# Another order of heads and channel groups by the column tiles of their weights, in a hybrid decoder layer on one core

## The chip, the cores and the metric

The kernel runs on one core of a Trainium2 chip. The metric is the time of one execution on the device in microseconds. A time of 2246.14 us is the median of three runs of the kernel before the change. The profile is of one more execution.

## What is computed

One layer takes 1024 new positions of one sequence and one new position each of 8 others, 2048 wide. With `h = rmsnorm(x) * (1 + scale) + shift`, where scale, shift and gate come from a conditioning vector through `w_ada`, it does this, cut from the reference:

```python
z = h @ w_in                                   # 2048 -> 8208 columns
b_a, c_a, h_a, g_a, qkv, g_b, beta_logit, alpha_logit = jnp.split(z, SPLIT_POINTS, axis=-1)
conv_out, new_a_buf = causal_depthwise_conv(c_a * h_a, conv_a_buf, conv_a_w)
y_a = b_a * conv_out * jax.nn.silu(g_a)
qkv_c, new_qkv_buf = causal_depthwise_conv(qkv, conv_qkv_buf, conv_qkv_w)
qkv_c = jax.nn.silu(qkv_c).astype(f32)
...
o, s = gated_delta_rule(q, k, v, g, beta, s0)
o = rmsnorm(o, o_norm_g).reshape(bsz, t, D_GDN).astype(x.dtype) * jax.nn.silu(g_b)
y = jnp.concatenate([y_a, o], axis=-1) @ w_out
return x + gate * y, new_a_buf, new_qkv_buf, s.astype(s0.dtype)
```

There are 8 channel groups of 128 columns (the first part, y_a) and 8 heads of 128 (the delta rule). Everything is in fp32 and the states are outputs too.

## The kernel before

**Columns.** A column tile is 128 columns of `w_in`, and its product over 2048 rows is one column of work. Group g needs four: C, H, gate and B, at 1024, 2048, 3072 and 0, plus 128 g. Head h needs four parts: k, q, v and gate, at 5120, 4096, 6144 and 7168, plus 128 h. All these bases are multiples of 1024, so all four columns of group or head i have the same place i modulo 8 within a block of eight tiles. In this text they are "of tile i". There are 64 such columns in each half.

**Halves.** The 1024 positions are done in two halves of 512; the second takes the 8 single positions along. In each half come the input products, then the output products with `w_out`, 16 column tiles. Half 0 begins with a ramp: while scale and shift are computed from `w_ada`, the first seven columns are multiplied as their inputs become ready. These are head 0's four and group 0's C, H and gate. Six of them are loaded two at a time in pieces of 128 KB (`add_pair`, L570), the seventh, the gate (`RONE`, L1364), as four pieces of 256 KB.

**A weight's way.** `Stream` (L557 and on) has one list, `todo`, of quads: 512 rows of one column, 256 KB, in runs of 512 bytes. For each quad the SP queue issues the load into `raw`; ACT rounds it to `whi`; POOL, or VectorE if POOL is busy, writes the rest `wlo`; then TensorE does three matmuls for each of its four tiles. Four raw buffers and four split ones (RAW, SPL, L387) let a load be issued up to eight quads ahead of its product. The order of `todo` is the order of the products.

**Heads.** A head's delta rule runs beside the products as a chain: preparation (`gdn_prep`, which loads `dA` by DMA), inversion (`gdn_invert`: ACT's `sp`, products, and through DRAM `ub` and `tb`, then 31 steps on VectorE), and application (`gdn_apply`, with `pb`, `u`, `st`, four chunks one after another). One head's inversion waits for the one before it, and so does its application. At most three heads have buffers for k and q.

**What sets the order of instructions.** The program is written out by a planner when it is built. `_Order` keeps an estimated time of every engine, tile and transfer; a generator that waits is resumed when the estimate says that its data are there, and its instructions are put at that place into the engines' queues. All queues then run in that order, whatever the true times are. Transfers are estimated by `_transfer` (L293): 210 GB/s for runs of 128 elements, for every column alike. The order of heads and groups is made by `order(half)` (L1338) from `GROUPS` and `APART`. Before the change, with C and H written CH and gate and B written GB, the columns are, in half 0 after the ramp: group 0's B, head 1, group 7 CH and GB, head 2, group 1 CH, head 3, group 1 GB, head 4, group 2 CH, head 5, group 2 GB, group 3 CH, head 6, group 3 GB, then head 7's four parts with two columns of groups 4 and 5 between them, then group 5 GB and group 6. In half 1: head 0, group 0 CH, head 1, group 0 GB, group 7 CH, head 2, group 7 GB, head 3, group 1, and then as in half 0.

**Gates.** `gate_chunks` (L1516) computes the third part of the `w_ada` product beside half 0's products, in steps at least `GATES` apart; its loads are `gw`, 256 KB each, on the same SP queue. A step was placed when its two tiles were estimated to have landed.

Of the kernel before, what the change touches and what calls it, by code (L numbers as in the profile page):

```python
# [11 lines left out]
ALU = mybir.AluOpType  # L12
# [4 lines left out]
P = 128  # L17
# [5 lines left out]
NH = 8  # L23
NC = 4
# [354 lines left out]
def _trunk(ctx, tc, nc, xT, w_in, w_ada, w_out, pack, consts, vecs, csq, ssm, yT, cap, cqp, ssp, cas, cqs, sss):  # L379
# [411 lines left out]

    solved, merged, recd = [0, 0], [0, 0], [0, 0]

    def gdn_prep(half, h, gp, t):
# [4 lines left out]
        g4 = {n: gt[n][:, h, :] for n in gt}  # L799
# [5 lines left out]
        SY.dma_start(dA[:], gcd[half, h * NC:(h + 1) * NC, :].partition_broadcast(P))  # L805
# [105 lines left out]
        yield LANDED  # L911
        cx["yc"] = yc

    def gdn_apply(half, h, gp, done, cx, kq, yt):
# [3 lines left out]
        g4 = {n: gt[n][:, h, :] for n in gt}  # L918
# [61 lines left out]
        for c in range(NC):  # L980
            col = slice(c, c + 1)
            oc = po[:, c * P:(c + 1) * P]
            zero = half == 0 and c == 0
            if zero:
                r = vn[:, c, :]
                G.memset(os_[:, c, :], 0.0)
            else:
                pks = ch_tile()
                mm(pks[:, :P], kT[c], st[h][:], start=True, stop=True)
                mm(pks[:, P:2 * P], qT[c], st[h][:], start=True, stop=True)  # L990
# [12 lines left out]
            pd = ch_tile()  # L1003
            mm(pd[:, :P], kt[:, c, :], u2[:], start=True, stop=True)
            if zero:
                V.tensor_copy(st[h][:], pd[:, :P])
            else:
                V.scalar_tensor_tensor(st[h][:], st[h][:], g4["egl"][:, col], pd[:, :P], ALU.mult, ALU.add)
            yield [st[h][:], u1[:], MARGIN]
            mm(oc, dA[:, c, :], u1[:], start=True, stop=True)  # L1010
        recd[half] = h + 1
        od.unpin(cx["v"])
        if half:
            SY.dma_start(ssp[h], st[h][:])


        yield [po[:]]
# [20 lines left out]
        done.append(h)  # L1038


    sample_done = []
# [296 lines left out]
    def order(half):  # L1338

        a = [("a", i) for i in GROUPS for _ in range(2)]
        every = (0, 1, 2, 3)
        r = [] if half == 0 else [("h", 0, every)]
        if half == 0:
            a.pop(0)
        for h in range(1, NH):
            for _ in range(APART[half][h - 1]):
                r.append(a.pop(0))
            if h < NH - 1:  # L1350
                r.append(("h", h, every))
                continue
            for part in every:
                r += [("h", h, (part,)), a.pop(0)]
        return r + a

    GROUPS = (0, 7, 1, 2, 3, 4, 5, 6)

    APART = ((1, 2, 1, 1, 1, 2, 1), (1, 2, 1, 2, 1, 2, 1))

    HCOLS, ACOLS = (5120, 4096, 6144, 7168), (1024, 2048, 3072, 0)
    ADA = 9

    RCOLS, RONE = ((ACOLS[0], ACOLS[1]), (HCOLS[0], HCOLS[1]), (HCOLS[2], HCOLS[3])), ACOLS[2]  # L1364
    for kp in range(NK // 2):
        for c in RCOLS:
            ws.add_pair(w_in, c, kp)
        if kp % 2:
            ws.add(w_in, RONE, (kp // 2,))
    for half in range(2):  # L1370
        seen = [0] if half == 0 else []
        for kind, i, *parts in order(half):
            if kind == "h":
                cols = [HCOLS[part] for part in parts[0]]
            else:
                cols = ACOLS[2 if half or i else 3:] if i in seen else ACOLS[:2]
                seen.append(i)
            for c in cols:
# [137 lines left out]
    def gate_chunks():  # L1516
# [11 lines left out]
        for f in range(NK):  # L1528
# [2 lines left out]
                od.pin(ps)  # L1531
            for i in (4 * f, 4 * f + 2):
                yield GATES
                yield [tiles[i][:], tiles[i + 1][:]]
                for k in range(i % 4 * 4, i % 4 * 4 + 8):
                    j = k % 4
                    mm(ps[32 * j:32 * j + 32, f % 4 * P:(f % 4 + 1) * P], sc[:, k, :],
                       tiles[f * 4 + k // 4][:, j * P:(j + 1) * P], cost=0.096 if k % 8 else 0.18,
                       start=(k < 4), stop=(k >= 12), tile_position=(0, 32 * j))
                tiles[i] = tiles[i + 1] = None  # L1540
                for j in (4, 5):
                    if i + j < 4 * NK:
                        load(i + j)
# [41 lines left out]
    for half in range(2):  # L1585
# [3 lines left out]
        with ExitStack() as pools:  # L1589
# [7 lines left out]
            def chain(h, half, queue, done, gp):  # L1597

                while len(queue) <= h or len(queue[h]["ready"]) < 2 or recd[half] < h - 1:
                    yield 0.2  # L1600
                t = queue[h]
                yield [t["kq"][:], MARGIN]
                cx = yield from gdn_prep(half, h, gp, t)
                yield from gdn_invert(half, h, gp, t["kq"], cx)
                yield from gdn_apply(half, h, gp, done, cx, t["kq"], t["gb"])

            def runner(zl, queue, done, gp, half):
                yield from gates(half, zl)
# [6 lines left out]
            def head(i, parts, pss=None):  # L1615
                for part in parts:
                    if part == 0:
                        while recd[half] < i - 2:
# [5 lines left out]
                    t = queue[i]  # L1624
# [4 lines left out]

            groups = {}  # L1630
            if half == 0:
                ys[0] = new_y()
                groups[0] = group_a(0, 0, blocks, ys[0], (ramp[0], ramp[1], ramp[6]))
                next(groups[0])
                next(groups[0])
                head(0, range(4), [r[0] for r in ramp[2:6]])
                od.spawn(conditions())
            pl = [mm_tile() for _ in blocks]
            for k in range(NK):
# [4 lines left out]
            for kind, i, *parts in order(half):  # L1644
                if kind == "h":
                    head(i, *parts)
                elif i not in groups:
                    ys[i] = new_y()
                    groups[i] = group_a(half, i, blocks, ys[i])
                    next(groups[i])  # L1650
                else:
                    rest = groups[i]
                    next(rest)
                    if i != GROUPS[-1] and (half or i):
                        next(rest)
            while len(done) < NH:
                od.advance()

# [5 lines left out]
            def split_y():  # L1664
                for kq in ROWS:
                    for k in range(4 * kq, 4 * kq + 4):
                        while k == GROUPS[-1] and not last:
# [14 lines left out]
                    next(splits)  # L1682
            splits = split_y()
            od.spawn(splits)
            next(rest)
            last.append(True)

            def load_x(m, a, b):
# [162 lines left out]
```

## Time and profile before

| what | before |
|---|---|
| median of 3 runs | 2246.14 us (2242.96 to 2247.1) |
| the profiled execution | 2246.98 us |
| its span, first to last instruction | 2245.2 us |
| TensorE busy | 2135.5 us (95%) |
| VectorE, ACT, POOL busy | 1255.9, 832.1, 841.7 us |
| moved by DMA | 299.66 MB, mean 133 GB/s |
| mean granted TensorE clock | 0.977 |

The page names engines PE (TensorE's matmuls), PEld (its weight loads, which overlap), DVE (VectorE), ACT, POOL and SP (the queue that issues most transfers). Matmuls are pipelined, so "busy" there includes overlapping. All engine operations are recorded by one helper line (L317) and all matmuls by another (L366), so rows are told apart by the tiles they write and read: `whi<-raw` is ACT's split, `raw<-in_w_in` a weight load, `mm<-hh,whi` a product, `tpt` and `cht` and `ot` are PSUM tiles of the heads' chain. A row of the waits has the engine and what it wrote, what ended the wait, and then the total in us, the number of times and the longest. A row of the stages has the stretch, the busy time of each engine with its number of instructions, the granted clock, the share of the DMA engines and the rate.

### The profile page before, as it was taken

Reading aid. Unit: us, or ns where it says so; the run is one execution under the profiler, and the core shown is the slowest. Engines: PE = TensorE matmul, PEld = TensorE weight load, DVE = VectorE, ACT = ScalarE, POOL = GpSimd, SP = SyncE. Lnnn points to the kernel's source line nnn. Section 1 sums busy time; section 2 is a strip of 40 time slices with the busy share of each in tenths; the row PEclk is TensorE's granted clock in tenths of the full one; section 3 lists DMA queues with packets and bytes.
Section 4 is the critical chain, followed back from the end, with each engine's and each line's share of the span. In section 5 each row is a group of like instructions: output and inputs, shape, how many; then the busy total and the mean of one; then the engine's idle time right before and its main releaser. Section 6 shows DMA issues by size and latency. Waiting matters only on the chain. (4 is left out here: it accounts for less than half of the span.)

```text
span 2245.2 us, 40456 instructions
## 1 busy us (share of the span) xinstructions
PE 2135.5 (95%) x15033; PEld 1872.1 (83%) x15033; DVE 1255.9 (56%) x3649; ACT 832.1 (37%) x1887; POOL 841.7 (37%) x815
## 2 busy tenths in 40 slices
PE   4799899999999999999998999999999999999997
PEld 3457767777777878888888989999999999998996
DVE  3225647657586576368324647667576554735645
ACT  3123423343443433343333333343433423334553
POOL 1122333343333444332434333444433444433444
PEclk9789999999999999999999999999999999999998
DMA  9684796766564667555543585855445575747776
GB/s 272 213 271 109 109 138 144 137 144 144 129 128 85 89 97 101 86 136 187 155 110 84 120 110 104 118 110 121 102 94 93 81 95 78 112 80 213 211 220 207
DMA packets 507319, 299.66 MB, mean 133 GB/s; under 512 B 37361, under 2 KB 486641, under 8 KB 507121
## 3 DMA queue, kind: packets, MB, share of 16 engines
q1 hardware_dynamic: 482352, 285.17, 60.2%
q10 hardware_dynamic: 24768, 11.90, 2.3%
q8 instruction: 118, 1.93, 0.4%
q14 instruction: 81, 0.66, 0.1%
HBM read 277.06 MB, written 19.94 MB: 132 GB/s over the span
## 5 line engine op out<-in xcount | busy, mean ns | idle before, releaser
L317 POOL TENSOR_TENSOR wlo<-raw,whi 128x512 fp32r<-128x512 f32 x543 | 722.5, 1332 | 1294.0 <-ACT whi L317 1154.8
L366 PE MATMUL mm<-hh,whi 128*128 128x264 f32 (+1 forms) x3008 | 978.9, 325 | 10.0 <-ACT whi L317 4.2
L366 PE MATMUL mm<-hl,whi 128*128 128x264 f32 (+1 forms) x3008 | 975.0, 324 | 1.9 <-DVE hl L317 1.8
L366 PE MATMUL mm<-hh,wlo 128*128 128x264 f32 (+1 forms) x3008 | 975.0, 324 | 0.1
L317 ACT ACTIVATE whi<-raw 128x512 fp32r<-128x512 f32 x672 | 419.9, 628 | 725.6 <-PE mm L366 447.2
L366 PEld LDWEIGHTS mm<-hh,whi 128*128 128x128 f32 x3008 | 572.0, 190 | 59.3 <-issue 8.3
L366 PEld LDWEIGHTS mm<-hl,whi 128*128 128x128 f32 x3008 | 572.5, 190 | 44.9 <-DVE hl L317 4.2
L366 PEld LDWEIGHTS mm<-hh,wlo 128*128 128x128 f32 x3008 | 572.6, 190 | 41.0 <-issue 1.4
L366 PE MATMUL mm<-yhi,wlo 128*128 128x512 f32 (+2 forms) x768 | 248.0, 323 | 4.8 <-DVE wlo L317 2.5
L366 PE MATMUL mm<-ylo,whi 128*128 128x512 f32 (+2 forms) x768 | 247.4, 322 | 0.3 <-DVE ylo L317 0.3
L366 PE MATMUL mm<-yhi,whi 128*128 128x512 f32 (+2 forms) x768 | 246.6, 321 | 0.8 <-ACT whi L317 0.7
L317 DVE TENSOR_TENSOR ob<-tb,xb 128x62 f32<-128x62 f32 (+30 forms) x992 | 200.5, 242 | 14.6 <-DMA tb<-ub 14.6
L317 DVE TENSOR_TENSOR xb<-xb,ob 128x62 f32<-128x62 f32 (+30 forms) x992 | 186.6, 228 | 0.0
L366 PEld LDWEIGHTS mm<-yhi,wlo 128*128 128x128 f32 x768 | 145.4, 189 | 19.1 <-POOL wlo L317 3.6
L366 PEld LDWEIGHTS mm<-ylo,whi 128*128 128x128 f32 x768 | 145.4, 189 | 12.7 <-issue 0.8
L366 PEld LDWEIGHTS mm<-yhi,whi 128*128 128x128 f32 x768 | 145.4, 189 | 12.4 <-ACT whi L317 1.2
L317 DVE TENSOR_TENSOR wlo<-raw,whi 128x512 fp32r<-128x512 f32 x129 | 97.9, 765 | 78.3 <-ACT whi L317 76.9
L317 DVE SCALAR_TENSOR_TENSOR kq<-zr,pk,kq 128x512 f32<-128x512 f32 x96 | 108.4, 1129 | 3.4
L317 DVE SCALAR_TENSOR_TENSOR res<-mm,ga,xr 128x512 f32<-128x512 f32 (+2 forms) x48 | 27.3, 568 | 112.3 <-PE mm L366 99.5
L366 PE MATMUL tpt<-wat,sc 128*32 128x256 f32 (+1 forms) x640 | 46.8, 408 | 39.6 <-DMA wat<-in_w_ada 36.0
L317 DVE TENSOR_TENSOR acc<-acc,sqt 128x512 f32<-128x512 f32 (+3 forms) x75 | 54.1, 723 | 29.9 <-ACT sqt L317 28.2
L366 PEld LDWEIGHTS tpt<-wat,sc 128*32 128x32 f32 x640 | 17.9, 124 | 62.0 <-DMA wat<-in_w_ada 23.2
(401 smaller groups left out, 1989.6 us busy)
## 6 DMA issues: line engine op xcount, KB each, us to landing
raw<-in_w_in SPq DMA_DIRECT2D x488, 256.0 KB, 4.7
raw<-in_w_out SPq DMA_DIRECT2D x160, 256.0 KB, 3.1
wat<-in_w_ada SPq DMA_DIRECT2D x64, 512.0 KB, 8.7
gw<-in_w_ada SPq DMA_DIRECT2D x64, 256.0 KB, 6.0
tb<-ub ACTq DMA_DIRECT2D x16, 512.0 KB, 7.3
raw<-in_w_in SPq DMA_DIRECT2D x48, 128.0 KB, 7.0
sl<-in_ssm SPq DMA_DIRECT2D x12, 512.0 KB, 6.4
x1s<-in_xT SPq DMA_DIRECT2D x16, 260.0 KB, 4.8
```

The source lines that it names most:

```text
L317: r = f(*args, **kw)
L366: r = self.pe.matmul(out, lhsT, rhs, **kw)
```

## The change

Five edits go together. `_transfer` takes 66 GB/s for columns of tiles 0 and 7 of `w_in`, and so every estimate behind it. `order(half)` is written out by parts. A group's CH, gate and B, and a head's four parts, are now placed one by one, and the heads come in the order 2, 1, 3, 4, 7, 5, 0, 6 in both halves. The ramp takes head 2 and group 2 in place of head 0 and group 0 (`FIRSTS`). A gate step is placed `LAND`, 2.0 us, after its tiles are estimated to have landed. In `gdn_apply`, the wait for the head's gate part stands at the start and no longer ahead of the last transposition. The other edits pass the head's number (`hd`) beside its place in the order (`h`).

In half 0 the columns are now, after the ramp: 2B, head 1, 1CH, head 3, 1 gate, head 4, 1B, 7k, 3CH, 7q, 3 gate, 7v, 3B, 7 gate, head 5, 0k, 4CH, 0q, head 6, 0v, 4GB, 0 gate, 5CH, 0CH, 5GB, 0 gate of the group, 6CH, 0B, 6 gate, 7CH, 6B, 7GB (k, q, v are a head's; C, H, B a group's). In half 1: head 2, 2CH, head 1, 0CH, head 3, 0 gate, 2GB, 0B, 1CH, head 4, 7k, 1GB, 7q, 3CH, 7v, head 5, 7 gate, 3GB, 0k, 4CH, 0q, 4GB, 0v, head 6, 0 gate of the head, group 5, 7CH, 6CH, 7 gate, 6GB, 7B.

```diff
+SLOW = (0, 7)
 def _transfer(src, dst):
     n = _size(dst) * dst.shape[0]
+    if src.tensor.name == "in_w_in" and int(src.offset) % 8208 // P % 8 in SLOW:
+        return n * 4 / 66e3
...
-        while recd[half] < h:
+        while recd[half] < h or len(cx["ready"]) < 4:
             yield 0.2
...
-        while len(cx["ready"]) < 4:
-            yield 0.3
         yield [os_[:], yt[:, :HT], MARGIN]
...
     def order(half):
+            r = a(2, 2) + h(1) + a(1, 0) + h(3) + a(1, 1) + h(4) + a(1, 2) + h(7, 0) + a(3, 0) + h(7, 1) + a(3, 1)
...
-    GROUPS = (0, 7, 1, 2, 3, 4, 5, 6)
-    APART = ((1, 2, 1, 1, 1, 2, 1), (1, 2, 1, 2, 1, 2, 1))
+    FIRSTS = (2, 2)
+    HEADS = [i for kind, i, part in order(1) if (kind, part) == ("h", 0)]
+    LASTG = order(1)[-1][1]
...
-    RCOLS, RONE = ((ACOLS[0], ACOLS[1]), (HCOLS[0], HCOLS[1]), (HCOLS[2], HCOLS[3])), ACOLS[2]
+    ra, rh = (tuple(c + i * P for c in cols) for cols, i in zip((ACOLS, HCOLS), FIRSTS))
+    RCOLS, RONE = (ra[:2], rh[:2], rh[2:]), ra[2]
...
-                yield [tiles[i][:], tiles[i + 1][:]]
+                yield [tiles[i][:], tiles[i + 1][:], LAND]
```

How this moves instructions, at two places. First, ACT in half 0, from the first eviction of a group's C after the ramp to the second head's `sp`. `c_` and `gc` are evicted columns of a group, `zr` is one of a head, `whi` is a split, `xd` and `yc` are transfers of the head before. Before:

```order
L317 ACTIVATE c__2227<-mm 128x512
L317 ACTIVATE whi<-raw 128x512 x7
L317 DMA xd<-xb 128x128
L317 ACTIVATE whi<-raw 128x512
L317 ACTIVATE gc<-mm 128x512
L317 ACTIVATE whi<-raw 128x512
L317 DMA yc<-xd 128x4x32
L317 ACTIVATE sp<-kq 128x512
```

Now:

```order
L322 ACTIVATE c__2227<-mm 128x512
L322 ACTIVATE whi<-raw 128x512 x7
L322 DMA xd<-xb 128x128
L322 ACTIVATE whi<-raw 128x512
L322 ACTIVATE zr<-mm 128x512
L322 ACTIVATE whi<-raw 128x512
L322 DMA yc<-xd 128x4x32
L322 ACTIVATE sp<-kq 128x512
```

The number of splits ahead of `sp` is the same, nine; what was split before was group 7's columns, and is now group 1's and head 3's.

Second, POOL in half 1, from the gate part of the second head (`gbs`) to what follows the next group's C and H (`ua`). A `zr` copy belongs to a head's part, `ua`, `halo_a` and `nca` to a group's, `dA` and `sm` to a head's chain. Before:

```order
L317 COPY gbs<-y 128x8
L317 TENSOR_TENSOR wlo<-raw,whi 128x512 x13
L317 COPY ua<-halo_a 128x2
L317 TENSOR_TENSOR wlo<-raw,whi 128x512
L317 COPY halo_a<-ua 128x2
L317 COPY nca<-pk 128x8
L317 COPY nca<-ua 128x8
L317 TENSOR_TENSOR sm<-sm,nhalf 128x4
L317 TENSOR_TENSOR wlo<-raw,whi 128x512
L317 COPY zr<-halo 128x3
```

Now:

```order
L322 COPY gbs<-y 128x8
L322 TENSOR_TENSOR wlo<-raw,whi 128x512
L322 TENSOR_TENSOR sm<-sm,phalf 128x4
L322 TENSOR_TENSOR dU<-dA,sm 128x512
L322 TENSOR_TENSOR wlo<-raw,whi 128x512 x2
L322 COPY ua<-halo_a 128x2
L322 TENSOR_TENSOR wlo<-raw,whi 128x512
L322 COPY halo_a<-ua 128x2
L322 COPY nca<-pk 128x8
L322 COPY nca<-ua 128x8
L322 TENSOR_TENSOR wlo<-raw,whi 128x512 x2
L322 COPY zr<-halo 128x3
```

Before, group 0's gate and B and group 7's C and H stood together between two heads, 13 of their splits on POOL ahead of `ua`. Now only group 0's C and H do, and a column of head 3 follows them.

More of the change, by code (lines that the diff above doesn't have):

```diff
@@ L792, in _trunk, with gdn_prep @@
     solved, merged, recd = [0, 0], [0, 0], [0, 0]
-    def gdn_prep(half, h, gp, t):
+    def gdn_prep(half, hd, gp, t):
         kq, ready = t["kq"], t["ready"]
@@ L798, in gdn_prep @@
         qT = [kq[:, 1, c * P:(c + 1) * P] for c in range(NC)]
-        g4 = {n: gt[n][:, h, :] for n in gt}
+        g4 = {n: gt[n][:, hd, :] for n in gt}
         sm = gp.tile([P, 8, NC], F32, tag="sm", name="sm", bufs=3)
@@ L804, in gdn_prep @@
         dA = gp.tile([P, NC, P], F32, tag="dA", name="dA", bufs=2)
-        SY.dma_start(dA[:], gcd[half, h * NC:(h + 1) * NC, :].partition_broadcast(P))
+        SY.dma_start(dA[:], gcd[half, hd * NC:(hd + 1) * NC, :].partition_broadcast(P))
         junk = tp.tile([P, P], F32, tag="gv", name="junk", bufs=1)[:]
@@ L912, in gdn_invert, with gdn_apply @@
         cx["yc"] = yc
-    def gdn_apply(half, h, gp, done, cx, kq, yt):
+    def gdn_apply(half, h, hd, gp, done, cx, kq, yt):
         kT = [kq[:, 0, c * P:(c + 1) * P] for c in range(NC)]
         qT = [kq[:, 1, c * P:(c + 1) * P] for c in range(NC)]
-        g4 = {n: gt[n][:, h, :] for n in gt}
+        g4 = {n: gt[n][:, hd, :] for n in gt}
         ssk, ssq, rk2, nk, w, w2, sso, rs = (cx["sm"][:, i, :] for i in range(8))
         kt, dA, dU, yc = cx["kt"], cx["dA"], cx["dU"], cx["yc"]
-        while recd[half] < h:
+        while recd[half] < h or len(cx["ready"]) < 4:
             yield 0.2
@@ L1338, in order, with h, a @@
     def order(half):
-        a = [("a", i) for i in GROUPS for _ in range(2)]
-        every = (0, 1, 2, 3)
-        r = [] if half == 0 else [("h", 0, every)]
+        def h(i, *parts):
+            return [("h", i, part) for part in parts or range(4)]
+        def a(i, *parts):
+            return [("a", i, part) for part in parts]
         if half == 0:
[L1346 to L1355, printed above, removed]
-    GROUPS = (0, 7, 1, 2, 3, 4, 5, 6)
-    APART = ((1, 2, 1, 1, 1, 2, 1), (1, 2, 1, 2, 1, 2, 1))
+            r = a(2, 2) + h(1) + a(1, 0) + h(3) + a(1, 1) + h(4) + a(1, 2) + h(7, 0) + a(3, 0) + h(7, 1) + a(3, 1)
+            r += h(7, 2) + a(3, 2) + h(7, 3) + h(5) + h(0, 0) + a(4, 0) + h(0, 1) + h(6) + h(0, 2) + a(4, 1, 2)
+            r += h(0, 3) + a(5, 0) + a(0, 0) + a(5, 1, 2) + a(0, 1) + a(6, 0) + a(0, 2)
+            return r + a(6, 1) + a(7, 0) + a(6, 2) + a(7, 1, 2)
+        r = h(2) + a(2, 0) + h(1) + a(0, 0) + h(3) + a(0, 1) + a(2, 1, 2) + a(0, 2) + a(1, 0) + h(4)
+        r += h(7, 0) + a(1, 1, 2) + h(7, 1) + a(3, 0) + h(7, 2) + h(5) + h(7, 3) + a(3, 1, 2)
+        r += h(0, 0) + a(4, 0) + h(0, 1) + a(4, 1, 2) + h(0, 2) + h(6) + h(0, 3)
+        return r + a(5, 0, 1, 2) + a(7, 0) + a(6, 0) + a(7, 1) + a(6, 1, 2) + a(7, 2)
+    FIRSTS = (2, 2)
+    HEADS = [i for kind, i, part in order(1) if (kind, part) == ("h", 0)]
+    LASTG = order(1)[-1][1]
     HCOLS, ACOLS = (5120, 4096, 6144, 7168), (1024, 2048, 3072, 0)
     ADA = 9
-    RCOLS, RONE = ((ACOLS[0], ACOLS[1]), (HCOLS[0], HCOLS[1]), (HCOLS[2], HCOLS[3])), ACOLS[2]
+    ra, rh = (tuple(c + i * P for c in cols) for cols, i in zip((ACOLS, HCOLS), FIRSTS))
+    RCOLS, RONE = (ra[:2], rh[:2], rh[2:]), ra[2]
     for kp in range(NK // 2):
@@ L1370, in _trunk @@
     for half in range(2):
[L1371 to L1378, printed above, removed]
+        for kind, i, part in order(half):
+            for c in HCOLS[part:part + 1] if kind == "h" else (ACOLS[:2], ACOLS[2:3], ACOLS[3:])[part]:
                 ws.add(w_in, c + i * P, range(4))
@@ L1602, in chain @@
                 yield [t["kq"][:], MARGIN]
-                cx = yield from gdn_prep(half, h, gp, t)
+                cx = yield from gdn_prep(half, HEADS[h], gp, t)
                 yield from gdn_invert(half, h, gp, t["kq"], cx)
-                yield from gdn_apply(half, h, gp, done, cx, t["kq"], t["gb"])
+                yield from gdn_apply(half, h, HEADS[h], gp, done, cx, t["kq"], t["gb"])
             def runner(zl, queue, done, gp, half):
@@ L1617, in head @@
                     if part == 0:
-                        while recd[half] < i - 2:
+                        while recd[half] < len(queue) - 2:
                             od.advance()
@@ L1623, in head @@
                                       "gb": y, "ready": []})
-                    t = queue[i]
+                    t = queue[HEADS.index(i)]
                     if part == 2:
@@ L1631, in _trunk @@
             if half == 0:
[L1632 to L1636, printed above, removed]
+                g0 = FIRSTS[0]
+                ys[g0] = new_y()
+                groups[g0] = group_a(0, g0, blocks, ys[g0], (ramp[0], ramp[1], ramp[6]))
+                next(groups[g0])
+                next(groups[g0])
+                head(FIRSTS[1], range(4), [r[0] for r in ramp[2:6]])
                 od.spawn(conditions())
@@ L1643, in _trunk @@
             od.spawn(runner(zl, queue, done, gp, half))
-            for kind, i, *parts in order(half):
+            for kind, i, part in order(half)[:-1]:
                 if kind == "h":
-                    head(i, *parts)
-                elif i not in groups:
+                    head(i, (part,))
+                    continue
+                if part == 0:
                     ys[i] = new_y()
                     groups[i] = group_a(half, i, blocks, ys[i])
[L1650 to L1655, printed above, removed]
+                next(groups[i])
             while len(done) < NH:
@@ L1666, in split_y @@
                     for k in range(4 * kq, 4 * kq + 4):
-                        while k == GROUPS[-1] and not last:
+                        while k == LASTG and not last:
                             yield 0.3
@@ L1684, in _trunk @@
             od.spawn(splits)
-            next(rest)
+            next(groups[LASTG])
             last.append(True)
```

14 lines of the change are left out of this document (7 added, 7 removed).

## The prediction

> **What bounds the kernel now.** The page comes first: is there an engine that is nearly always busy, and where is it not?
>
> ```profile
> span 2245.2 us, 40456 instructions
> PE 2135.5 (95%) x15033; PEld 1872.1 (83%) x15033; DVE 1255.9 (56%) x3649; ACT 832.1 (37%) x1887; POOL 841.7 (37%) x815
> PE   4799899999999999999998999999999999999997
> PEclk9789999999999999999999999999999999999998
> GB/s 272 213 271 109 109 138 144 137 144 144 129 128 85 89 97 101 86 136 187 155 110 84 120 110 104 118 110 121 102 94 93 81 95 78 112 80 213 211 220 207
> ```
>
> TensorE sets the time: it is idle for 2245.2 - 2135.5 = 109.7 us only, and the change takes no matmul away. So all that can be won is in those idle stretches, and in the clock, which is granted in part after a stretch without work. Next the table by stages, with cuts chosen where the idle time lies.
>
> ```profile
> core 0: us, PE busy (x) PEld busy (x) DVE busy (x) ACT busy (x) POOL busy (x), PEclk, DMA share, GB/s
> 0.00:210.00 210.00, 160.46 (x1082) 100.61 (x1083) 66.47 (x122) 52.90 (x86) 37.25 (x43) 0.88 0.79 227
> 250.00:340.00 90.00, 77.96 (x462) 59.64 (x460) 44.91 (x166) 25.54 (x58) 28.61 (x26) 0.92 0.95 126
> 340.00:1180.00 840.00, 834.15 (x4553) 673.27 (x4553) 502.52 (x1476) 318.28 (x705) 328.74 (x302) 1.00 0.60 125
> 1180.00:1245.00 65.00, 56.30 (x456) 55.68 (x455) 25.77 (x40) 24.40 (x58) 26.44 (x29) 0.95 0.37 90
> 1300.00:1345.00 45.00, 40.32 (x351) 39.22 (x350) 16.73 (x32) 15.18 (x41) 14.72 (x12) 0.92 0.89 100
> 1345.00:1800.00 455.00, 453.08 (x3958) 447.46 (x3957) 298.54 (x959) 174.85 (x449) 182.72 (x196) 1.00 0.56 103
> 1800.00:1830.00 30.00, 27.84 (x220) 27.62 (x219) 19.98 (x92) 7.25 (x14) 12.86 (x13) 0.94 0.57 102
> 1870.00:1900.00 30.00, 26.48 (x201) 26.30 (x200) 12.03 (x24) 12.70 (x42) 13.16 (x11) 0.89 0.62 69
> 2020.00:2245.00 225.00, 206.21 (x1739) 199.14 (x1737) 118.72 (x267) 110.34 (x239) 100.12 (x80) 0.97 0.73 212
> ```
>
> Of the 109.7 us, 49.5 lie in the ramp (0 to 210) and 18.8 in the tail (from 2020). Between them five short stages lose 12.04 + 8.70 + 4.68 + 2.16 + 3.52 = 31.1 us, while the 1295 us of the two long rows (340 to 1180 and 1345 to 1800) lose 7.8. What are the five? The waits of TensorE alone name what ended each:
>
> ```profile
> PE tpt L366 <- DMA wat<-in_w_ada: 36.0, 10, 18.6
> PE mm L366 <- DMA gw<-in_w_ada: 6.9, 2, 6.6
> PE tpt L366 <- DVE v L317: 6.3, 1, 6.3
> PE tpt L366 <- ACT sp L317: 5.0, 1, 5.0
> PE cht L366 <- ACT pb L317: 4.2, 1, 4.2
> PE cht L366 <- DVE u L317: 4.1, 2, 3.5
> PE mm L366 <- ACT zr L317: 2.3, 2, 2.1
> PE mm L366 <- DVE y L317: 2.2, 1, 2.2
> ```
>
> None of them is a wait for weights, so one more step back is needed: what were ACT and VectorE waiting for? The timeline of ACT from 297 us, and then one row each from the waits of 1190 to 1260, 1290 to 1350, 1790 to 1830 and 1870 to 1900:
>
> ```profile
> 297.78 0.63 ACT L317 ACTIVATE whi<-raw 128x512 fp32r<-128x512 f32 x1 [3.79 <-DMA raw<-in_w_in]
> ...
> 323.85 0.63 ACT L317 ACTIVATE whi<-raw 128x512 fp32r<-128x512 f32 x1 [0.60 <-DMA raw<-in_w_in]
> 326.01 0.63 ACT L317 ACTIVATE sp<-kq 128x512 fp32r<-128x512 f32 x1 [1.54 <-DMA xd<-xb]
> ```
>
> ```profile
> DVE dA L317 <- DMA dA<-gcd: 10.0, 1, 10.0
> ...
> ACT pb L317 <- DMA raw<-in_w_in: 7.3, 1, 7.3
> ...
> DVE ob L317 <- DMA tb<-ub: 6.0, 1, 6.0
> ...
> DVE dA L317 <- DMA dA<-gcd: 5.3, 1, 5.3
> ```
>
> Counted along the list of loads, the eight splits from 297.78 to 323.85 are the last two columns of group 7, one per 26.07 / 7 = 3.72 us, and sp, which TensorE waits for, stands behind them on ACT. In all five stages columns of tile 0 or 7 are being loaded, and something else queues behind them: on ACT in program order (sp, pb), or among the transfers (gw, dA, tb). The issues by window, 284 to 312 (tile 7), 340 to 395 (tile 2) and 1188 to 1216 (tile 0), show the difference directly:
>
> ```profile
> raw<-in_w_in SPq DMA_DIRECT2D x8, 256.0 KB, 12.2
> ...
> raw<-in_w_in SPq DMA_DIRECT2D x15, 256.0 KB, 4.8
> ...
> raw<-in_w_in SPq DMA_DIRECT2D x9, 256.0 KB, 12.7
> ```
>
> The same 256 KB land after 12.2 and 12.7 us from tiles 7 and 0, after 4.8 us from tile 2. So the planner's 210 GB/s, 262144 bytes in 1.25 us, is wrong for two tiles in eight. A fast quad (256 KB) takes about 0.96 us, an estimate from the 272 GB/s of the page's first slice.
>
> **The change part by part.** These rows are still needed: TensorE in 1000 to 1100 and in 770 to 900, the ramp's loads from 88 to 190, and the sp of the next head.
>
> ```profile
> 1000.00:1100.00 100.00, 100.00 (x434) 81.16 (x433) 67.86 (x115) 37.84 (x62) 31.11 (x24) 1.00 0.57 178
> ...
> 770.00:900.00 130.00, 130.00 (x642) 105.66 (x641) 83.98 (x277) 46.08 (x108) 60.07 (x57) 1.00 0.74 99
> ...
> raw<-in_w_in SPq DMA_DIRECT2D x34, 128.0 KB, 7.4
> raw<-in_w_in SPq DMA_DIRECT2D x6, 256.0 KB, 11.6
> ...
> 398.66 0.62 ACT L317 ACTIVATE sp<-kq 128x512 fp32r<-128x512 f32 x1
> ```
>
> A quad is 12 matmuls of 100 / 434 = 0.230 us, 2.77 us. A slow column thus takes 4 x 3.72 = 14.9 us to load against 11.1 us of products. One alone falls 3.8 us behind, which the eight quads that are loaded or split ahead (22.2 us) cover. Four in a row fall 15 us behind and, worse, hold what queues behind them.
>
> Step 1, the five stages. Their runs of 4 to 6 slow columns (group 7 in half 0; head 0 and group 0, then group 0 and group 7, at the start of half 1) become runs of one, or of two. The splits also move later on ACT, because the estimate now says when slow raws land. What goes is at least the idle time, 31.1 us. On top comes clock: one minus the granted clock, times the stage, is 7.2 + 3.3 + 3.6 + 1.8 + 3.3 = 19.2 us, part of it during the idle time itself. Ends 31.1 and 50.3; I take half of the clock, midway between the ends: 40.7 us.
>
> Step 2, the ramp. Six of its seven columns come as 128 KB loads (7.4 us median, next to 512 KB loads of w_ada), which look hardly slower for tile 0; the seventh, the group's gate column, as four quads (11.6 us; of the six in that row three are the gate column's and three the next slow column's). Each quad holds the queue for 3.72 - 0.96 = 2.8 us too long. The first lies ahead of the slices with 109 GB/s, where time is lost anyway; the other three delay the wat tiles for which TensorE waits, and the ramp's last product: 3 x 2.8 = 8.3 us. Ends: 0, if other loads fill the ramp, and 17.4 + 4 = 21 us, all of wat's waits but the first (36.0 - 18.6) and the last quad. I take 8.3, the row nearest.
>
> Step 3, what comes back. The ramp's tile 0 was cheap; now all sixteen slow columns of each half are in the stream, 32 in place of 25. The single slow columns of before are head 7's: in half 0 (770 to 900) four with no idle time at all, in half 1 four with 2.16 + 3.52 = 5.7 us, 1.4 each, through tb and dA. At 1.4 for each of half 1's sixteen, 22.7 us; at none, 0. With the transfers of tb and dA now planned at the true rate I take half: 11.4 us. Pairs of slow columns at the end of half 0 (7C 7H, 6B, 7G 7B) lag 2 x 8 x (3.72 - 2.77) - 4 x (2.77 - 0.96) = 8 us plus a landing of 4.8, under 22.2: nothing.
>
> Step 4, the rest. LAND delays gate products by 2 us a step; who waits for them is half 0's output, which comes after all of the half's columns, so it costs nothing. It moves the 6.9 us wait away, which is within step 1. gdn_apply now waits for the gate part before it starts instead of near its end; in the new order every head's fourth part stands before its apply rows, so nothing waits. Head and group names only permute. TensorE's filler rows in the output stage are untouched.
>
> Sum: 40.7 + 8.3 - 11.4 = 37.6 us off the profiled execution's 2246.98 gives 2209.4; the runs' median lies 0.84 below that execution, so **2208.5 us**.
>
> A rule weighed: the Trainium skill, "DMA: Bandwidth & Descriptors" (Specifications, and Latency and other measured facts), gives 512 B as the size from which transfers run at line rate, and ties slow HBM reads to the pitch of the rows. All columns here have 512 B runs and one pitch, so by that rule tile 0 is no slower than tile 2, and steps 1 and 2 are worth nothing. The rows of 12.2 against 4.8 us contradict it.
>
> **The rivals.**
>
> *Column order does not matter.* The slow loads belong to the time (start of a half, gw traffic) and not to the tile: the stalls stay, 2246 us. For it: the worst stages do stand at the starts. Against: head 7's loads in mid-half, and tile 0 in half 1 without any gw, are slow too. The rule of the Trainium skill quoted above would give this case. Chance 0.06.
>
> *The heads' chain sets half 0.* One head's inversion follows another's; sp to sp took 398.66 - 326.01 = 72.65 us over five columns. The new order puts the first inversions five, five, five, then six or seven columns apart, so three cycles have no room. If each is late by a wait like sp's 5.0 plus 1.7 of clock, 20 us come back: 2228. Against: from 340 to 398 that same spacing cost TensorE no wait. Chance 0.10.
>
> *Slow columns meet the heads' transfers.* It ends on the other side. With 32 slow columns spread over all sixteen heads, tb and dA land behind one nearly everywhere. A meeting cost 2.16 to 3.52 us of idle time and 1.8 to 3.3 of clock, 5.4 on average; steps 1 and 2 bring 49, so it decides from nine meetings. With 14 it gives 49 - 76, 27 us slower: 2273. For it: both meetings of before hit single columns. Against: they were planned at 1.25 us a quad, and half 0's four cost nothing. Chance 0.07.
>
> **How the numbers follow.** The forecast has 0.77. Its low end, all clock and four ramp quads with little coming back, is 2246 - 50.3 - 11 + 3 = 2188; its high end, idle time alone, no ramp gain and 22.7 back, is 2246 - 31.1 + 22.7 = 2237. That also holds the chain's 2228; outside are the two other rivals and a small part of the forecast. About 0.2% (4.5 us) is what a measurement of this kernel can tell from no change: faster by more 0.87 (forecast and chain), the same 0.06, slower 0.07.
>
> **What would show it.** Right: TensorE idle below 15 us between ramp and tail, no wait of ACT for raw in runs, ramp's last product some 8 us earlier, tile 2's ramp quads near 7 us. Wrong: step 1, if 256 KB loads of tile 0 or 7 stay at 12 us or tile 2's rise; step 2, if the first column after the ramp starts where it did; step 3, if DVE waits for tb and dA are many and end in waits of TensorE. Idle time before sp in half 0 would point to the chain.

## The result, and the profile after

| what | before | after |
|---|---|---|
| median (four runs each, side by side) | 2244.96 us | 2209.97 us (2208.98 to 2215.43) |
| ratio, 95% interval | 1 | 0.9842 (0.9825 to 0.986) |
| the profiled execution | 2246.98 us | 2215.43 us |
| its span | 2245.2 us | 2213.4 us |
| idle time of TensorE in it | 109.7 us | 86.0 us |

The kernel is 35 us faster; 37.6 were forecast. The profiled execution of after lies 5.5 us above its median, so a stage of it can be a few us too long.

The page of after, the lines that were shown of before:

```profile
span 2213.4 us, 40425 instructions
PE 2127.4 (96%) x15033; PEld 1865.4 (84%) x15033; DVE 1254.3 (57%) x3664; ACT 829.3 (37%) x1887; POOL 823.4 (37%) x800
PE   5889999999999999999999999999999999999997
PEclk9899999999999999999999999999999999999998
GB/s 291 246 292 58 129 160 144 135 124 144 116 133 89 95 97 94 73 143 187 151 120 101 117 128 113 111 111 107 97 100 82 95 100 96 87 90 230 212 219 202
```

The dip to 8 in the fifth slice, where group 7 was loaded, is gone, and the clock's third slice has 9 in place of 8. For the account the spans are cut where the stages begin: at the first column after the ramp, the first output column of half 0, the first column of half 1 and its first output column. First before, then after:

```profile
0.00:210.00 210.00, 160.46 (x1082) 100.61 (x1083) 66.47 (x122) 52.90 (x86) 37.25 (x43) 0.88 0.79 227
210.00:981.80 771.80, 753.92 (x4269) 601.66 (x4268) 472.68 (x1514) 295.36 (x696) 304.49 (x291) 0.99 0.65 116
981.80:1169.30 187.50, 187.50 (x843) 153.35 (x842) 94.55 (x155) 62.41 (x102) 64.03 (x49) 1.00 0.54 161
1169.30:2026.40 857.10, 833.85 (x7161) 823.72 (x7160) 509.91 (x1601) 316.86 (x777) 338.75 (x355) 0.99 0.56 99
2026.40:2245.20 218.80, 199.81 (x1685) 192.74 (x1684) 112.31 (x260) 104.61 (x228) 97.16 (x78) 0.97 0.74 216
```

```profile
0.00:202.40 202.40, 157.00 (x1083) 100.71 (x1084) 66.26 (x122) 53.15 (x86) 36.74 (x43) 0.92 0.82 236
202.40:967.20 764.80, 755.06 (x4269) 601.30 (x4268) 472.49 (x1523) 289.57 (x691) 285.86 (x277) 0.99 0.65 116
967.20:1158.20 191.00, 188.04 (x843) 152.90 (x842) 96.16 (x159) 64.77 (x107) 68.91 (x50) 1.00 0.52 160
1158.20:1996.60 838.40, 828.24 (x7162) 818.72 (x7161) 508.02 (x1606) 317.02 (x777) 331.91 (x351) 1.00 0.59 102
1996.60:2213.40 216.80, 199.06 (x1685) 191.78 (x1683) 111.33 (x257) 104.78 (x228) 99.94 (x79) 0.97 0.74 218
```

The second column is the length of the stage. Ramp 7.6 us shorter, half 0's products 7.0 shorter, half 0's output 3.5 longer, half 1's products 18.7 shorter, the end 2.0 shorter: 31.8 together. Between ramp and tail TensorE is idle for 9.74 + 2.96 + 10.16 = 22.9 us, before 17.88 + 23.25 = 41.1. More than the 15 that the prediction expected stays.

TensorE's largest waits in that part of after:

```profile
PE mm L371 <- DVE y L322: 3.8, 2, 2.1
PE mm L371 <- DVE wlo L322: 3.0, 2, 1.7
PE cht L371 <- DVE acc L322: 2.5, 1, 2.5
PE mm L371 <- DVE ua L322: 1.8, 1, 1.8
...
PE cht L371 <- ACT pb L322: 1.4, 1, 1.4
```

The waits for v, for sp and for gw (6.3, 5.0 and 6.9 us) are gone or under 1 us. What of ACT's waits for raw and VectorE's for dA and tb, which lay behind them? From 200 to 2100 us, before and after:

```profile
ACT whi L317 <- DMA raw<-in_w_in: 52.3, 21, 5.5
...
DVE dA L317 <- DMA dA<-gcd: 19.3, 4, 10.0
DVE ob L317 <- DMA tb<-ub: 14.6, 7, 6.0
```

```profile
ACT whi L322 <- DMA raw<-in_w_in: 75.4, 30, 4.7
...
DVE ob L322 <- DMA tb<-ub: 2.6, 1, 2.6
DVE dA L322 <- DMA dA<-gcd: 1.3, 1, 1.3
```

The waits for dA and tb have all but vanished, 33.9 us to 3.9. ACT's waits for raws did not: they rose from 52.3 to 75.4 us. The loads of tile 7 are as slow as before; only little that TensorE needs stands behind them now. The loads of after, by window: 929 to 955 (two columns of tile 7, one behind the other, 12.4), 589 to 598 (one column of tile 0 by itself, 6.8, where the run of before had 12.7), 215 to 240 (fast tiles), and the ramp's from 88 to 190, now of tile 2:

```profile
raw<-in_w_in SPq DMA_DIRECT2D x8, 256.0 KB, 12.4
...
raw<-in_w_in SPq DMA_DIRECT2D x4, 256.0 KB, 6.8
...
raw<-in_w_in SPq DMA_DIRECT2D x8, 256.0 KB, 5.5
...
raw<-in_w_in SPq DMA_DIRECT2D x29, 128.0 KB, 6.1
raw<-in_w_in SPq DMA_DIRECT2D x7, 256.0 KB, 4.4
```

### The profile page after: what moved, and what is told of

Read it like the earlier page. It is cut to its first block, busy times and chain, and to the rows that moved or that the text cites. A ratio compares the mean times of both kernels' runs of the same rounds, so it can differ in the third digit from the quotient of the medians.

```text
span 2213.4 us, 40425 instructions
## 1 busy us (share of the span) xinstructions
PE 2127.4 (96%) x15033; PEld 1865.4 (84%) x15033; DVE 1254.3 (57%) x3664; ACT 829.3 (37%) x1887; POOL 823.4 (37%) x800
## 5 line engine op out<-in xcount | busy, mean ns | idle before, releaser
L322 POOL TENSOR_TENSOR wlo<-raw,whi 128x512 fp32r<-128x512 f32 x528 | 707.0, 1341 | 1279.5 <-ACT whi L322 1105.2
L322 DVE TENSOR_TENSOR ob<-tb,xb 128x62 f32<-128x62 f32 (+30 forms) x992 | 195.6, 237 | 2.6 <-DMA tb<-ub 2.6
L322 DVE TENSOR_TENSOR xb<-xb,ob 128x62 f32<-128x62 f32 (+30 forms) x992 | 196.2, 238 | 0.0
L322 DVE TENSOR_TENSOR wlo<-raw,whi 128x512 fp32r<-128x512 f32 x144 | 110.1, 769 | 133.8 <-ACT whi L322 133.0
L371 PEld LDWEIGHTS mm<-yhi,whi 128*128 128x128 f32 x768 | 144.5, 188 | 12.7 <-ACT whi L322 1.6
L322 DVE SCALAR_TENSOR_TENSOR kq<-zr,pk,kq 128x512 f32<-128x512 f32 x96 | 99.6, 1037 | 3.4
L322 DVE SCALAR_TENSOR_TENSOR res<-mm,ga,xr 128x512 f32<-128x512 f32 (+2 forms) x48 | 27.3, 568 | 109.1 <-PE mm L371 101.8
L322 DVE SCALAR_TENSOR_TENSOR rt<-cht,gt_neg,v 128x128 f32<-128x128 f32 x56 | 19.6, 350 | 81.0 <-PE cht L371 81.0
```

The lines of the kernel that those rows point to most:

```text
L322: r = f(*args, **kw)
L371: r = self.pe.matmul(out, lhsT, rhs, **kw)
```

## The experiments

The theory is that of the prediction: the order counts, since it breaks the runs of slow columns. The rival that the first runs were made for: the estimate counts, since it decides what the planner writes behind a split. In the table, the median and its ratio to the runs of before beside it (their medians lie from 2244.96 to 2247.59 us), and then the lengths in us of the stages in the profiled execution, cut as above.

| kernel | median, us | ratio to before | ramp | half 0 | its output | half 1 | end |
|---|---|---|---|---|---|---|---|
| before | 2244.96 | 1 | 210.0 | 771.8 | 187.5 | 857.1 | 218.8 |
| after | 2209.97 | 0.9842 (0.9825 to 0.986) | 202.4 | 764.8 | 191.0 | 838.4 | 216.8 |
| estimate only | 2230.26 | 0.9928 (0.991 to 0.9946) | 221.8 | 758.3 | 186.5 | 841.2 | 219.1 |
| estimate, 256 KB only | 2226.56 | 0.9911 (0.9895 to 0.9927) | 213.7 | 758.4 | 186.5 | 843.4 | 218.8 |
| order only | 2237.30 | 0.9956 (0.9938 to 0.9973) | 201.2 | 772.9 | 191.8 | 848.5 | 218.0 |
| half loads, before | 2240.38 | 0.9973 (0.9962 to 0.9984) | 212.9 | 768.0 | 187.4 | 854.7 | 218.7 |
| half loads, after | 2235.97 | 0.9948 (0.993 to 0.9966) | 200.0 | 775.9 | 190.3 | 846.5 | 219.2 |
| old order, ramp 2 | 2224.71 | 0.9904 (0.9889 to 0.9918) | 198.5 | 773.2 | 186.7 | 843.0 | 218.4 |
| the same, no LAND | 2234.19 | 0.9946 (0.9931 to 0.996) | 200.5 | 779.1 | 186.7 | 843.3 | 218.9 |
| slow together | 2298.02 | 1.023 (1.0214 to 1.0246) | 199.6 | 845.4 | 195.2 | 837.3 | 221.9 |
| ramp on tile 0 | 2233.03 | 0.9939 (0.9925 to 0.9953) | 218.9 | 772.6 | 187.9 | 836.7 | 217.0 |
| no waits | 2231.25 | 0.9935 (0.9919 to 0.995) | 197.1 | 786.5 | 190.7 | 835.3 | 216.7 |
| no waits, head 6 later | 2212.44 | 0.9851 (0.9835 to 0.9867) | 199.0 | 766.4 | 190.9 | 837.0 | 217.4 |
| head 6 later | 2203.49 | 0.9814 (0.9797 to 0.983) | 199.9 | 758.9 | 191.0 | 835.1 | 215.9 |

**The estimate alone.** To the kernel before:

```diff
 def _transfer(src, dst):
     n = _size(dst) * dst.shape[0]
+    if src.tensor.name == "in_w_in" and int(src.offset) % 8208 // P % 8 in SLOW:
+        return n * 4 / 66e3
```

> The order of the columns as in the kernel before; only the planner's estimate is changed (tiles 0 and 7 at 66 GB/s). If it is the order that counts (a run of four to six slow columns falls behind and holds the transfers behind it, whatever the planner knows), then the stages that lose time through gw, dA and tb stay, and at most the waits of sp and pb behind the splits on ScalarE go: 2228 to 2247 us, and 256 KB loads of tiles 0 and 7 stay at 12 us. If the estimate alone does it (nothing stands behind a split that waits for its raw any more), 2205 to 2220 us.

2230.26 us, within the theory's range, but not for its reason: half 0 is 13.5 us shorter and half 1 15.9, with the old order and its runs, while the ramp is 11.8 longer.

**The order alone.** The changed kernel without those two lines.

> The new order, the ramp on tile 2, with the old estimate of 210 GB/s for every tile. If the order counts, nearly all of the gain stays: 2208 to 2222 us, where up to 11 us come back because splits of single slow columns again stand on ScalarE ahead of work that others wait for. If the estimate does it, only the ramp's 8 us stay: 2232 to 2240 us.

2237.30 us, as the rival had it: the ramp's gain of 8.8 us and hardly more. Half 0 does not get shorter at all, half 1 by 8.6. So in the changed kernel the estimate is worth 27.3 us (2237.30 to 2209.97), on the kernel before 15.3. What came in place of the old waits: TensorE's largest wait from 201 to 2015 us, then VectorE's from 200 to 2100.

```profile
PE cht L366 <- DVE xc L317: 12.0, 4, 5.5
```

```profile
DVE xc L317 <- DMA yc<-xd: 34.0, 6, 10.7
...
DVE dA L317 <- DMA dA<-gcd: 25.3, 8, 7.3
DVE ob L317 <- DMA tb<-ub: 4.9, 2, 4.3
```

The spread slow columns do meet the heads' transfers, 14 times here in dA and yc, and it costs. This is the rival "slow columns meet the heads' transfers". With the true rate in the planner VectorE's waits for yc, dA and tb are 6.4 us together (2.5, 1.3 and 2.6): the work that needs them is written later.

**Half loads**, on the kernel before and on the order alone:

```diff
-                self.todo.append(((col, kq), [(0, 4, src)]))
+                cuts = (0, 2, 4) if w is w_in and col // P % 8 in (0, 7) else (0, 4)
+                self.todo.append(((col, kq), [(i, j, src[:, i:j, :]) for i, j in zip(cuts, cuts[1:])]))
```

> The kernel before, its order and its estimate; only the 256 KB loads of tiles 0 and 7 are issued as two of 128 KB (two blocks of 128 rows each in place of four). The ramp's 128 KB loads of tile 0 looked hardly slow. If the slowness belongs to these tiles in the form of 256 KB, it goes: the five stages and the ramp's gate quads get fast, 2195 to 2215 us. If it belongs to the tile whatever the form, or to the time at which the loads run, nothing changes: 2240 to 2250 us.

> The new order with the 256 KB loads of tiles 0 and 7 as two of 128 KB, and the old estimate of 210 GB/s for every tile. If the form of the load makes the slowness, what the 32 slow columns still cost goes too (forecast at 11.4 us, at most 23): 2190 to 2207 us. If the form does not matter, it is the same as the new order without the estimate: 2208 to 2222 us.

2240.38 and 2235.97 us. The first is as the second reading had it. The second lies outside both ranges, which were written before the order alone had run; it is the same as that kernel (2237.30), as the second reading said. So the form of the load is not the cause. From 284 to 312 us in the kernel before with half loads, columns of tile 7 again:

```profile
raw<-in_w_in SPq DMA_DIRECT2D x13, 128.0 KB, 8.9
```

13 pieces of 128 KB in 28 us, where before had 8 of 256 KB: no faster. So tile 0's 128 KB loads in the ramp were probably slow as well, and only hidden among other loads (7.4 us before and 6.1 now). The 5 us that the first of the two gained are not explained by this; its waits of TensorE lack the one for sp.

**The old pattern with everything else**: estimate, ramp on tile 2, moved waits; in half 0 heads 2, 1, 3, 4, 5, 0, 6, 7 and groups 2, 7, 1, 3, 0, 4, 5, 6 in the places of before, half 1 as before.

> The changed kernel with the pattern of the order before: runs of four slow columns in half 0 (group 7, then head 0) and of six and four at the start of half 1; the ramp on tile 2 and the estimate of 66 GB/s stay. Theory of the prediction (a run falls behind by 3.8 us a column and holds what queues behind it): the stages' idle time stays for the most part, 2225 to 2241 us. Rival, from the run with the estimate alone (the runs cost little once nothing is placed behind a split whose raw is late): that run's 2230 less the 19.4 us by which its first column after the ramp starts later than the changed kernel's (221.8 against 202.4): 2207 to 2215 us.

2224.71 us, just below the theory's range, and hardly better than the estimate for 256 KB alone (2226.56, below). The ramp is 15.2 us shorter than there, and half 0, which now has tile 0's seven other columns too, four of them in one run, is 14.8 longer. From here the new order brings 14.7 us by the medians (2209.97), less than half of what the theory had. The two profiled executions are only 6.4 apart: 8.4 won in half 0, 4.6 in half 1 and 1.6 at the end, 3.9 lost in the ramp and 4.3 in half 0's output.

Is it by breaking runs of slow columns that the order wins? The end of half 0 and the start of half 1 in this kernel, and TensorE's largest wait in half 0:

```profile
940.00:971.70 31.70, 23.98 (x111) 19.48 (x110) 16.29 (x26) 14.78 (x35) 10.36 (x8) 0.89 0.18 52
1158.40:1340.00 181.60, 172.20 (x1400) 170.10 (x1398) 92.02 (x248) 63.89 (x144) 62.43 (x68) 0.97 0.57 107
```

```profile
PE tpt L371 <- DVE os__9042 L322: 6.4, 1, 6.4
```

At the start of half 1 it is: 9.4 us idle with six slow columns in a row, 0.8 in after (its row stands below). At the start of half 0 it is too: 5.6 us idle from 198.5 to 340 us, 0.7 in after from 202.4 to 340. But the largest piece of half 0, 7.7 us idle from 940 us on, is no wait for a weight. No product of `w_in` starts between 948.5 and 959.5 us: the last column is not written before all heads are done (`while len(done) < NH`), and TensorE waits for the last head's output `os`. After, where head 6 is last, has 0.3 us idle from 935 us on, and the kernel with the estimate for 256 KB, with the order of before, nothing from 940. So the order wins in half 0 at least as much by when the heads end as by the runs. Why the last head is late here stays open.

**Slow columns together**: the new order with 0 and 1, and 7 and 3, exchanged.

> The changed kernel's order with the names exchanged so that tiles 0 and 7 stand in the places of 1 and 3: a run of eleven slow columns at the start of half 0 and five in a row at the start of half 1, with the estimate. Theory of the prediction: eleven columns fall 42 us behind, of which 22 are covered, so 20 us and the transfers held behind them come back: 2228 to 2245 us. Rival (a column's pace with all that TensorE does between is 15 us in half 0, as long as a slow column's load of 14.9): 2207 to 2217 us.

2298.02 us, 88 more than after and outside both. But the run itself ran well: its first six columns took from 211.7 to 296.6 us, 14.1 each, where half 0 of before has 13.5 for a column of any tile. The loss comes behind it: the stage from 356 to 420, TensorE's and ACT's waits for the first head, and the issues from 240 to 360.

```profile
356.00:420.00 64.00, 41.39 (x278) 29.47 (x277) 37.93 (x227) 13.55 (x30) 5.80 (x6) 0.63 0.46 122
```

```profile
PE tpt L371 <- ACT sp L322: 10.8, 2, 10.0
...
ACT sp L322 <- DMA xd<-xb: 15.5, 2, 14.2
```

```profile
raw<-in_w_in SPq DMA_DIRECT2D x31, 256.0 KB, 11.8
...
ub<-dU ACTq DMA_DIRECT2D x4, 16.0 KB, 9.3
```

The first head's chain makes several trips through DRAM, and each stands behind slow loads; 16 KB take 9.3 us, where the median of all such transfers of before is 3.8. And there is a gate in the order of writing that the prediction had left out (the heads' gate from here on; it has to do neither with the clock nor with `gate_chunks`): `head` does not write a new head's first column before the recurrence of the third head before it is written (`while recd[half] < len(queue) - 2: od.advance()`). The fourth head's column stood there until 419 us, and meanwhile the rest of the chain was written without products of `w_in` between (none from 372.6 to 419.4 us): 22.6 us idle in the stage at a clock of 0.63. From 630 to 685 us the same happens once more:

```profile
630.00:685.00 55.00, 41.68 (x211) 31.78 (x210) 39.51 (x131) 19.92 (x42) 9.33 (x13) 0.76 0.44 112
```

**The ramp on tile 0**: tiles 0 and 2 exchanged in the new order, `FIRSTS = (0, 0)`.

> The changed kernel with tiles 0 and 2 exchanged: the ramp on tile 0, tile 2's columns in the places of tile 0. By the prediction's step 2 the ramp is 8.3 us longer, and 11 slow columns fewer stand in the stream: 2212 to 2219 us. If the estimate of 66 GB/s, which in the ramp holds for the 128 KB loads too, makes the ramp on tile 0 as long as in the run with the estimate alone (first column at 222 in place of 202): 2225 to 2232 us.

2233.03 us; the ramp is 16.5 us longer than after's, not 8.3, and half 0 is 7.8 longer although it has fewer slow columns. The second reading was the nearer; the time lies 1 us above its range. And the estimate for 256 KB loads alone, on the kernel before:

```diff
+    if _size(dst) == 512 and src.tensor.name == "in_w_in" and int(src.offset) % 8208 // P % 8 in SLOW:
+        return n * 4 / 66e3
```

> The kernel before with the estimate of 66 GB/s for its 256 KB loads alone; the ramp's 128 KB loads stay at 210 GB/s. If the estimate cost the run with the estimate alone 12 us in the ramp (first column at 221.8 in place of 210.0) through the 128 KB loads, these come back: 2214 to 2222 us. If it did so through the gate column's 256 KB loads, it stays: 2227 to 2233 us.

2226.56 us, just under the second reading's range: 3.7 of the 12 us come back by the medians, though 8.1 in the ramp of the profile; the two intervals overlap. Two stages, before and then this kernel, show what the estimate does to the two worst places without any change of order:

```profile
210.00:340.00 130.00, 117.96 (x647) 92.27 (x645) 69.66 (x213) 45.62 (x106) 43.63 (x41) 0.95 0.79 115
...
1169.30:1350.00 180.70, 166.39 (x1385) 164.11 (x1384) 95.02 (x276) 65.55 (x152) 65.03 (x70) 0.96 0.56 103
```

```profile
213.70:340.00 126.30, 123.08 (x638) 96.00 (x637) 64.48 (x142) 44.50 (x102) 43.95 (x42) 1.00 0.81 121
1158.60:1340.00 181.40, 171.83 (x1395) 169.91 (x1394) 91.66 (x248) 64.10 (x144) 62.24 (x68) 0.97 0.56 107
```

At the start of half 0 the idle time falls from 12.0 to 3.2 us, though the same four columns of tile 7 are loaded there, hardly faster: from 287 to 314 us

```profile
raw<-in_w_in SPq DMA_DIRECT2D x7, 256.0 KB, 11.1
```

At the start of half 1, where six slow columns follow each other, 14.3 only falls to 9.6; in after, from 1158.2 to 1340, it is 0.8:

```profile
1158.20:1340.00 181.80, 180.96 (x1546) 179.37 (x1545) 107.33 (x302) 70.01 (x162) 70.89 (x83) 1.00 0.55 113
```

**The moved waits.** The changed kernel with both put back:

```diff
-                yield [tiles[i][:], tiles[i + 1][:], LAND]
+                yield [tiles[i][:], tiles[i + 1][:]]
...
-        while recd[half] < h or len(cx["ready"]) < 4:
+        while recd[half] < h:
```

> The changed kernel without its two moved waits: gate products wait for their tile without the 2 us on top, and a head's apply rows wait for the gate part near their end, as before. Step 4 has them at nothing: 2206 to 2214 us. If the 2 us keep gate products from waiting for gw, the 6.9 us wait of before is back: 2214 to 2222 us.

2231.25 us, 21 more than after; neither had it. The rows of every engine are the same with `gdn_apply`'s wait at either place, so it is LAND alone. The loss is in half 0, and a large piece of it lies where head 6, the last in the order, stands at the heads' gate, from 660 to 680 us. In the kernel without the waits and in after:

```profile
660.00:680.00 20.00, 12.29 (x50) 8.85 (x49) 14.46 (x77) 5.86 (x14) 3.10 (x6) 0.66 0.32 58
```

```profile
660.00:680.00 20.00, 17.46 (x86) 14.10 (x85) 15.33 (x56) 10.04 (x30) 5.61 (x8) 0.97 0.53 113
```

50 matmuls in 20 us, nearly all of one head's chain, one after another: no product of `w_in` starts between 661.6 and 679.9 us, where the longest such stretch of after is 4 us. The clock makes it worse: by the Trainium skill ("TensorE: Matmul & The Clock Gate", Part 1) the gate grants half or all of the clock, so a mean of 0.66 would be an estimated 13.6 of the 20 us at half; the rows show the mean alone. If it is the heads' gate, more room for that chain must bring the loss back, with the waits still away:

```diff
-            r += ... h(5) + h(0, 0) + a(4, 0) + h(0, 1) + h(6) + h(0, 2) + a(4, 1, 2)
-            r += h(0, 3) + ...
+            r += ... h(5) + h(0, 0) + a(4, 0) + h(0, 1) + a(4, 1) + h(0, 2) + a(4, 2)
+            r += h(6) + h(0, 3) + ...
```

> The changed kernel without its two moved waits (2231 us), with head 6's columns three places later in half 0, after the last of group 4. Theory: what cost 20 us there is the gate of the heads: a new head's first column is not written before the recurrence of the third head before it, so the rest of that head's chain is written without products between, and TensorE runs empty (7.7 us idle and a clock of 0.66 between 660 and 680 us). With 45 us more for that chain it goes: 2208 to 2217 us. Rival (the moved waits act elsewhere, on gw): 2226 to 2234 us.

2212.44 us: 18.8 come back, as the heads' gate has it. The same on the changed kernel:

> The changed kernel with head 6's columns three places later in half 0. In the changed kernel the same gate costs little: from group 4's hidden columns to its last one TensorE loses some 9 us (2.6 + 3.0 + 1.6 + 2.1). If the gate is what is left there: 2202 to 2208 us. If not, no change: 2208 to 2214 us.

2203.49 us, as the heads' gate has it, and 6.5 under after: the fastest kernel of this study, each of its runs below each run of after. Between these two LAND is still worth 9.0 us, 7.5 of them in half 0. Is that so with the old pattern?

> The old pattern with the ramp on tile 2 and the estimate (2224.7 us), without the 2 us ahead of the gate products. The run with the estimate alone, which has no such 2 us, needed 758 us from the ramp's end to the output stage of half 0, this pattern with them 773. If the 2 us only shift when heads meet their gate, for the worse here: 2205 to 2214 us. If they are what keeps the gate products from waiting for gw: 2225 to 2235 us.

2234.19 us: LAND is worth 9.5 us there too, so it is no accident of the new order, and the first reading was wrong. But gw stands in the list of TensorE's waits of neither of the two kernels, and in the new order it has 0.7 us with LAND and 1.8 without, so the reason given with the other reading does not hold either. Why LAND brings 9 us stays open.

Set side by side, these kernels tell more than each alone; all have the estimate and the ramp on tile 2:

| order | without LAND | with LAND | LAND brings |
|---|---|---|---|
| old pattern | 2234.19 | 2224.71 | 9.5 |
| new | 2231.25 | 2209.97 | 21.3 |
| new, head 6 later | 2212.44 | 2203.49 | 9.0 |

With head 6 out of the heads' gate the new order is worth nearly the same with and without LAND, 21.2 and 21.8 us, and LAND the same with either order (the runs of before beside them differ by up to 2.6 us). The changed kernel loses 6.5 us of that at the heads' gate, and without LAND 18.8, so that only 2.9 us of the order's gain are left there, which is inside the intervals of the two runs.

## Why the prediction was right, point by point

The sum was near, 37.6 against 35.0 us; its terms were less so, and that they met is in part luck. By stage it said 8.3 for the ramp, 15.6 for half 0 (12.04 + half of 7.2), and for half 1 25.1 less the 11.4 of step 3, 13.7. The profiles have 7.6, 7.0 less 3.5 in the output, and 18.7 with 2.0 at the end. So half 0 brought far less than forecast and half 1 more. And LAND, which the sum has at nothing, carries half 0: without it the changed kernel is 0.65% faster than before, some 15 us, and its half 0 14.7 us longer (786.5 against 771.8).

**What bounds the kernel: right.** TensorE's idle time between ramp and tail fell by 18.2 us, and the two worst of the five stages changed when only the estimate for tiles 0 and 7 did (12.0 to 3.2 and 14.3 to 9.6 us). That tile 7 is slow in another place and in another form too is shown (12.4 us after, halves no faster), and the last section has all eight tiles. "Column order does not matter" is refuted from both sides, by 14.7 us for the new order and by the 88 us of the slow columns together. The rule that was weighed (the Trainium skill, "DMA: Bandwidth & Descriptors", Specifications, and Latency and other measured facts), 512 bytes and the pitch of the rows, can't tell these tiles from the others, and the runs do.

**Step 1: the place right, the cause half wrong.** "Their runs of 4 to 6 slow columns become runs of one, or of two" was to remove the idle time, with the estimate as an addition. It is the other way round. The estimate alone takes 13.4 us off half 0 and 13.7 to 15.9 off half 1; the order alone nothing and 8.6. The working that failed is "14.9 us to load against 11.1 us of products". A column's pace is not its products: half 0 of before has 57 columns in 771.8 us, 13.5 each with the heads' and gates' work between. On that average a slow column falls 1.4 us behind, not 3.8, and four of them stay far inside the 22 us of cover. What cost time was not the lag but what stood behind the late raws in queues that can't be reordered: sp, pb, dA, gw. There the order helps second, where slow columns are many, at the start of half 1 (9.4 us idle with the old pattern and everything else, 0.8 after) and less at the start of half 0 (5.6 and 0.7). The clock's share can't be told apart.

**Step 2: right in size, for a reason that is partly wrong.** 7.6 us in the profile, 8.8 for the order alone. But the ramp's 128 KB loads of tile 0 seem to have been slow too. The 0.96 us for a fast quad, estimated from a stretch of other loads, is too short: the last section has 1.5 to 2.2. Nor is the gain free: with the old pattern half 0 gave back 14.8 of 15.2 us, 7.7 of them idle at the last head's end.

**Step 3: the middle of two ends, and both ends exist.** The prediction put 11.4 us on meetings of slow columns with tb and dA. With the estimate VectorE's waits for them are 3.9 us in all, so nothing came back that way, and half 1 gained 5 more than forecast. Without it they are 30.2 us, with 34.0 for yc beside, and only 8 of the 35 us of gain are left. The rival's mechanism is real; the edit in `_transfer` is what kept it away.

**Step 4: wrong on LAND, right on the rest.** `gdn_apply`'s wait changes no row. LAND, "it costs nothing", brings 9 us, and 21 where the heads' gate lies close. Nor was gw's wait what it moved: the kernel without LAND has 1.8 us of it, not 6.9. The step asked only who waits for the gates' output, and not what else stands beside the gate products in TensorE's queue.

**The heads' chain** had 0.10. Half 0 of the new order hangs on it: as the rival said, cycles have no room there. More room for one of them brings 6.5 us in after and 18.8 with LAND gone, and with the slow columns together two stages at the heads' gate have 36 us of idle time (22.6 and 13.3). The prediction looked for it in waits for sp. It acts through `recd` instead: TensorE's queue is written empty of products. In the kernel without the waits the rows of the waits name only the chain's own short steps there, 2.2 us the longest; what shows is a stage with few matmuls and a low clock.

**What was to show it.** Right were the ramp's end (7.6 us earlier) and tile 2's ramp quads (4.4 us). The idle time stayed at 22.9 us, not under 15. The sign against step 1, that 256 KB loads of tile 0 or 7 stay at 12 us, came for tile 7 (12.4) while the kernel got faster, since their landing was not what the time hung on. "No wait of ACT for raw in runs" was the wrong sign: those waits rose by 23 us while the kernel got faster.

## What to carry to other kernels

Where a planner or a hand writes in-order queues, a wrong duration for one kind of load can cost more than the order of the loads: here correcting it alone brought 15 to 19 us, moving the loads alone 8. Find the loads whose landing differs from their price, correct the price first, and only then move them. Compare a load with the pace of its whole stage, other work included, not with its own products. And look for gates in the order of writing (a buffer that must come free before the next item is written): near such a gate, a shift of 2 us in something unrelated was worth 21, of which 9 came without the gate as well.

## What the runs showed of the hardware

Column tiles 0 and 7 modulo 8 of a matrix with rows of 32,832 bytes are read one quad per 3.72 us, where 178 GB/s, the rate from 1000 to 1100 us, would need 1.47, although every tile has runs of 512 bytes and the same pitch. In the trace of after, a 256 KB load that was issued at least 2 us before the one ahead of it had landed lands 4.1 us after that one if it is of tile 0 and 3.9 if of tile 7 (medians of 40 and 53 loads); for the other six tiles it is 1.5 to 2.2. How long after its issue such a load lands differs with its company: 6.8 us for a column of tile 0 by itself, 12.7 in the run of before. For pieces of 128 KB it is no better (8.9 us for tile 7). The DMA engines are busy meanwhile: in the rows of the prediction a share of 0.95 at 126 GB/s where tile 7 is loaded (250 to 340 us), 0.57 at 178 GB/s from 1000 to 1100. Small transfers beside them are late as well, 16 KB after 9.3 us. Which part of the memory or of the engines makes the difference was not tried.
